# A diffusion layer on one Trainium2 core: the mixers' output product in seven products, and twelve first products ahead

## The chip, the cores and the metric

The kernel runs on one core of a Trainium2 chip. Its engines work from queues of their own: TensorE (PE) multiplies matrices, VectorE (DVE) and ScalarE (ACT) work on tiles element by element, GpSimd (POOL) adds some tiles and issues some transfers, SyncE (SP) issues most transfers. Engines wait for each other on semaphores. The metric is the device time of one execution in microseconds. Before the change it is 2686.76 us, the median of three runs (2683.47 to 2690.48).

## The reference, cut to what matters

One layer over 1024 latent tokens and 256 context tokens, all of width 1024: a half-step SwiGLU feed-forward (FFN), two token mixers side by side (short convolution and attention), merged by gates and multiplied by an output matrix, and a second FFN.

```python
x = x + 0.5 * ml[2] * swiglu(modulate(rms_norm(x, norm1_g), ml[0], ml[1]), ffn1_w_in, ffn1_w_out)
...
hx = modulate(rms_norm(x, norm2_g), ml[3], ml[4])
bg_l, cg_l, vc_l, q_l, k_l, v_l, gt_l = jnp.split(hx @ w_in, SPLITS, axis=-1)
...
x = x + ml[5] * ((g_conv * (y_conv @ w_bc) + g_attn * (o_attn @ w_ba)) @ w_out)
x = x + 0.5 * ml[8] * swiglu(modulate(rms_norm(x, norm3_g), ml[6], ml[7]), ffn2_w_in, ffn2_w_out)
return rms_norm(x, final_g)
```

`ml[0]` to `ml[8]` are nine vectors of modulation, `silu(c) @ w_mod + b_mod`, cut in nine. The context tokens go through the first FFN and the mixers' keys and values with the same weights.

## The kernel before, in words

**Layout and precision.** Activations lie transposed, 128 channels on the partitions and tokens along the row, in halves of 512 tokens: C0 and C1. Every factor of a matmul is split in a high and a low part, and three matmuls (high by high, high by low, low by high) make up one product of 128 x 128 by 128 x 512. ScalarE's cast makes the high part, DVE's subtraction the low one (`split`), so every operand costs one operation of each.

**Seven products for eight.** The large products with 1024 input channels (`Winograd`, L466) take a pair of column blocks of the weights, two halves of the inputs and two halves of the tokens, and form the four results from seven products of sums, in the order 1, 2, 6, 7, 4, 5, 3. `product(i)` takes one left part (the sums of weights, made by POOL; tiles s1 to s3 and raw, split into wl) and four right parts r(i) (the sums of normed inputs, made by DVE): 4 x 3 = 12 matmuls into one bank ps. `norm0` (L503) makes r1 and r2 from C0; `norm1` (L530) makes r6 and r5 from C1, then, in its last three steps, the right parts of products 7, 4 and 3 ("late" operands: each a `keep` of four tiles). `keep` is a cast on ScalarE and a subtraction on DVE.

**Starting ahead.** Products 1 and 2 need only C0. So `start` (L661) computes the first sums u and c of the first 9 pairs (AH2 for the mixers, AH3 for the second FFN; 12 for the first, through `start_together`), one pair after another, while the norm of C1 is made. Two pairs stay in the chip, the others are written to memory (`put_aside`, tiles uc and ucd, which have four buffers in the pool of weights, tag wh) and loaded again by `fetch` (L727) one pair ahead, into tiles u and c of the pool of small tiles (`ttile`, 11 buffers for everything temporary of 128x512). With one step of `norm1` for each pair (two for the first), all nine, the late ones too, are run within `start`. `second` (L743) adds products 6, 7 and 4, with calls for steps that are left (`run(self.late, 4)`); `third` (L755) adds 5 and 3.

**Row products.** The FFNs' second matrices go through `row_products` (L795): again seven products, each over all 11 pairs of hidden rows (tiles hid, rh, rl), into four banks at a time. When a product ends, `add` adds its four banks to x on DVE, at once.

**Modulation beside it.** `later_mod` (L262) multiplies the vectors that are needed later on DVE, from tiles rawm; its steps are run between pairs (`STEPS`, `late_steps`). After the last load it lets four (WAIT) and six steps pass idle before and after the accumulator is split (tiles macc, acch, accl).

**The mixers' end.** `merge(j, ch)` (L1640) multiplies the attention's output (`o_parts`, split in whole rows of 1024 by `split_output`, L1544: tiles oh and ol) by column block j of `w_ba` and gates it. It splits the merged rows into mh and ml. Then a loop over both halves and eight column blocks of `w_out` (L1714 to L1739) multiplies plainly: 8 x 3 = 24 matmuls for each block and half, into one bank, added to x by one operation on DVE. Each block is loaded and split once for each half of the tokens. Behind it `fast`, the second FFN's `Winograd`, starts (`norm0` within the loop's last blocks, `start` at L1841).

**What sets the order.** A scheduler that simulates the engines' timelines orders each engine's queue. Instructions issued while `strict[0]` is true, and matmuls marked `pinned`, keep their program order. Each queue is then worked in order, so that what is late at the head of DVE's or ScalarE's queue holds up everything behind it.

Of the kernel before, what the change touches and what calls it, by code (L numbers as in the profile page):

```python
# [49 lines left out]
def tile_dit_layer(  # L50
# [211 lines left out]
    def later_mod(m, halves=(0, 1), streams=None):  # L262
# [3 lines left out]
        for half in halves:  # L266
# [32 lines left out]
            yield  # L299
# [166 lines left out]
    class Winograd:  # L466
# [26 lines left out]
        def modulated(self, out, k, ch, pr):  # L493
            dve.tensor_mul(out=out, in0=self.xs(k, ch), in1=pr)
            self.shifted(out, k)

# [6 lines left out]
        def norm0(self, in_place=False):  # L503
# [8 lines left out]
            for i in range(2):  # L512
                for k in range(4):
                    h = self.h0[k][:, i]
                    self.modulated(h, k + 4 * i, C0, pr)
                    self.keep(1 + i, k, h)
                yield

# [51 lines left out]

        def lefts(self, pairs, side_from):

            def cols(src):
                t = wpool.tile([P, SLOT], F32, tag="raw", name=uniq("raw"), bufs=3)
                load(t[:].rearrange("p (k n) -> p k n", n=P), src.rearrange("(k p) n -> p k n", p=P))
                return t[:, :512], t[:, 512:]
# [9 lines left out]
            def parts(src):  # L586
                tag = "wh" if self.side_from and self.n_left in WH else "wl"
                self.n_left += 1
                t = wpool.tile([P, 2, 512], F32R, tag=tag, name=uniq(tag), bufs=W_BUFS)
                split(src, t[:, 0], t[:, 1], self.lo_eng)  # L590
                return t
# [11 lines left out]
            else:  # L603
                for a, _ in pairs[:n]:
                    yield from map(parts, cols(a))
# [689 lines left out]
    def after1(i, k):  # L1295
# [23 lines left out]
        if i == 3 and k in (0, 4):  # L1319
            run(norms2, 1)  # L1320
# [605 lines left out]
```

## Time and profile before

| | us |
|---|---|
| median of three runs | 2686.76 |
| the profiled execution | 2688.7 |
| its span, from first to last instruction | 2686.9 |
| PE busy | 2643.4 |
| weight loads of PE (PEld) busy | 2236.0 |
| DVE busy | 2007.1 |
| ScalarE busy | 1166.1 |
| POOL busy | 521.3 |

The program's stages lie in the profile so: first FFN's first product from about 30 us, its second product from 680, the mixers' products from 895, attention to 1850, the merges and the output product to 2054, then the second FFN. A page gives the busy time and its share of the span for each engine. A row of a timeline has the start, the length, the engine, the line, the operation, the tile written and the tiles read, how many alike follow each other, and in brackets the idle time before and what ended it. A row of waits names who waited, then after the arrow the tile that it waited for, and the sum, the count and the longest. All instructions have the line of one helper, so tiles and operations tell them apart. Matmuls overlap: one of 512 columns shows a duration near 390 ns, while the next starts much sooner.

### The profile page before, as it was taken

What the parts mean: (1) busy time and instruction counts of PE and PEld (TensorE: products, weight loads), DVE (VectorE), ACT (ScalarE), POOL (GpSimd) and SP (SyncE); (2) the same over time, 40 slices, a digit from 0 to 9 for tenths busy, and PEclk for the clock granted to TensorE, in tenths of its full rate; (3) what the DMA queues carried; (4) which work ended last, traced back from release to release, by engine and by line L of the source; (5) the groups of instructions that cost most, each with busy time, mean ns of one, the idle gap of its engine ahead of it and who ended that gap; (6) DMA issues with size and microseconds to landing.
All of it is one profiled execution on the core that took longest, in us unless ns stands there. A gap on an engine that the chain in (4) does not pass through costs nothing.

```text
span 2686.9 us, 37399 instructions
## 1 busy us (share of the span) xinstructions
PE 2643.4 (98%) x13593; PEld 2236.0 (83%) x13593; DVE 2007.1 (75%) x3356; ACT 1166.1 (43%) x2317; POOL 521.3 (19%) x409
## 2 busy tenths in 40 slices
PE   8999999999999999999999999999999999999998
PEld 5788898888788877888999888877888888888888
DVE  5888888786887889877488666775458875667875
ACT  6633543333454632333244666674236333334543
POOL 1244012121110044232033111000001533230200
PEclk9999999999999999999999999999999999999998
DMA  7655653346973445433213211002524543228731
GB/s 267 236 180 166 223 184 124 109 130 240 293 169 102 149 137 165 134 114 116 97 48 103 95 62 49 24 25 78 167 85 146 184 145 99 83 90 305 165 83 63
DMA packets 369920, 364.84 MB, mean 136 GB/s; under 512 B 27830, under 2 KB 261448, under 8 KB 369736
## 3 DMA queue, kind: packets, MB, share of 16 engines
q1 hardware_dynamic: 360712, 345.17, 39.0%
q0 software_dynamic: 9024, 17.30, 4.0%
q8 instruction: 106, 1.74, 0.3%
q14 instruction: 78, 0.64, 0.1%
HBM read 296.30 MB, written 66.06 MB: 135 GB/s over the span
## 4 chain that ended last, share of the span: by engine, by line
PE 88%; DVE 6%; DMA 2%; ACT 2%; issue 1%; SPq 1%; POOL 0%; DVEq 0%; ACTq 0%; POOLq 0%
PE ps L88 73%; PE po L88 7%; PE pt L88 7%; DMA rawm<-in_w_mod_dram 1%; DVE macc L88 1%; DVE wl L88 1%; SPq L88 1%; DVE xb L88 0%; DVE r L88 0%; ACT r L88 0%; DMA raw<-in_ffn_w_in_dram 0%; DMA xtok<-in_ctx_dram 0%; DVE ol L88 0%; DVE x L88 0%; DVE pts L88 0%
## 5 line engine op out<-in xcount | busy, mean ns | idle before, releaser
L88 PE MATMUL ps<-r,wl 128*128 128x512 f32 x5232 | 1213.4, 392 | 11.6 <-ACT wl L88 6.8
L88 PEld LDWEIGHTS ps<-r,wl 128*128 128x128 f32 x5232 | 983.9, 189 | 220.0 <-ACT wl L88 9.0
L88 ACT CAST wl<-s 128x512 fp32r<-128x512 f32 x256 | 158.0, 620 | 338.3 <-PE ps L88 266.6
L88 POOL TENSOR_TENSOR s<-raw 128x512 f32<-128x512 f32 x64 | 92.4, 1444 | 993.8 <-PE ps L88 346.6
L88 ACT CAST wl<-raw 128x512 fp32r<-128x512 f32 x286 | 176.4, 619 | 250.0 <-PE ps L88 160.6
L88 DVE TENSOR_TENSOR wl<-raw,wl 128x512 fp32r<-128x512 f32 x284 | 202.6, 717 | 68.3 <-ACT wl L88 64.7
L88 DVE TENSOR_TENSOR wl<-s,wl 128x512 fp32r<-128x512 f32 x256 | 231.8, 906 | 12.3 <-ACT wl L88 10.7
L88 POOL TENSOR_TENSOR s<-raw,s 128x512 f32<-128x512 f32 x64 | 99.8, 1560 | 363.9 <-DVE wl L88 354.4
L88 DVE SCALAR_TENSOR_TENSOR macc<-rawm,silu_c,macc 128x512 f32<-128x512 f32 x168 | 137.9, 837 | 9.5 <-DMA rawm<-in_w_mod_dram 9.1
L88 PE MATMUL ps<-wh,r 128*128 128x256 f32 x768 | 141.6, 285 | 0.0
L88 DVE TENSOR_TENSOR pts<-pt,pts 128x512 fp32r<-128x512 f32 x160 | 108.8, 687 | 39.4 <-ACT pts L88 38.4
L88 DVE TENSOR_TENSOR u<-u,ps 128x512 f32<-128x512 f32 x168 | 114.2, 680 | 28.5 <-PE ps L88 28.4
L88 DVE TENSOR_REDUCE m<-ps 128x1 f32<-128x512 f32 (+1 forms) x192 | 110.9, 596 | 31.0 <-PE ps L88 30.3
L88 ACT CAST pts<-pt 128x512 fp32r<-128x512 f32 x160 | 93.2, 593 | 88.7 <-PE pt L88 86.8
L88 ACT CAST rh<-hid 128x512 fp32r<-128x512 f32 x132 | 81.6, 621 | 112.2 <-PE ps L88 96.2
L88 PE MATMUL ps<-rh,wl 128*128 128x512 f32 x360 | 122.0, 389 | 0.0
L88 PEld LDWEIGHTS ps<-wh,r 128*128 128x128 f32 x768 | 120.6, 192 | 0.0
L88 ACT CAST wh<-raw 128x512 fp32r<-128x512 f32 (+1 forms) x88 | 69.3, 795 | 103.0 <-PE ps L88 79.5
L88 PE MATMUL po<-pts,vh 128*128 128x512 f32 x256 | 110.5, 437 | 1.5 <-ACT pts L88 1.5
L88 DVE TENSOR_TENSOR rl<-hid,rh 128x512 fp32r<-128x512 f32 x132 | 90.1, 686 | 26.5 <-ACT rh L88 13.5
L88 PE MATMUL ps<-wl,r 128*128 128x256 f32 x384 | 108.8, 283 | 0.0
L88 PE MATMUL ps<-kl,qs 128*128 128x512 f32 x384 | 105.3, 397 | 0.0
(298 smaller groups left out, 5068.1 us busy)
## 6 DMA issues: line engine op xcount, KB each, us to landing
raw<-in_ffn_w_in_dram SPq DMA_DIRECT2D x125, 512.0 KB
raw<-in_ffn_w_out_dram SPq DMA_DIRECT2D x72, 512.0 KB
rawm<-in_w_mod_dram SPq DMA_DIRECT2D x128, 256.0 KB
raw<-in_w_in_dram SPq DMA_DIRECT2D x61, 512.0 KB
hid<-hd SPq DMA_DIRECT2D x40, 512.0 KB
ws<-in_ffn_w_out_dram POOLq DMA_DIRECT2D x30, 512.0 KB, 6.6
ucd<-uc SPq DMA_DIRECT2D x22, 512.0 KB
hd<-c SPq DMA_DIRECT2D x38, 256.0 KB
```

What stands on the lines that cost most here:

```text
L88: inst = getattr(self.engine, name)(*args, **kw)
```

## The change

1. **The output product** becomes a `Winograd` of its own, `OutColumns`: four pairs of column blocks, seven products each, over merged rows instead of normed inputs. Its right parts are made as the merges end (`place`, `given`); products 1 and 2 of all four pairs are run first (`firsts`), then 6, 7 and 4 of all (`seconds`), then 5 and 3 (`fifth`, `last`). Each block of `w_out` is loaded once. The merges now run all of C0, then all of C1 in the order 0, 4, 1, 5, 2, 6, 3, 7, and load the columns of `w_ba` for each half. The squares of C0 are summed as they come.
2. **The start ahead**: AH3 goes from 9 to 12; `start` runs pairs in twos (product 1 of both, then product 2 of both), and the left parts are fetched in that order.
3. **Late operands**: of the last three steps of `norm1`, the first (product 7) still runs in `start`, the second (product 4) now stands behind product 6 and the third (product 3) behind product 4, both in program order (`late_operands`). The first FFN's `start` runs fewer of the steps of its norm ahead as well.
4. **Fetched first products** lie in the four wh buffers, in one transfer, and no longer in two small tiles.
5. **Row products**: the four banks of a product are added behind the first group's sums of the next product, in program order.
6. **Modulation**: no idle steps; a split stands behind the last load of its vector; `STEPS` is smaller, and the steps are run in thirds between the products of a pair.
7. **Attention's output** is split in halves of 512.

The core of the diff:

```diff
-STEPS = (0, 4, 4, 4, 5, 5, 5, 5, 5, 5, 5, 2, 12)
-WAIT = 4
+STEPS = (0, 3, 3, 3, 3, 3, 3, 4, 4, 4, 4, 1, 8)
 AH1, HALVES, WH = 12, 8, (4, 5, 6, 7, 12, 13, 14, 15, 20, 21, 22, 23)
-RESIDENT, AH2, AH3 = 2, 9, 9
+RESIDENT, AH2, AH3 = 2, 9, 12
...
-            for _ in range(WAIT):
-                yield
-            parts = []
-            for acc in accs:
+            for acc, v in zip(accs, streams):
                 ah, al = ttile("acch", dt=F32R), ttile("accl", dt=F32R)
                 split(acc, ah, al)
-                parts.append((ah, al))
-            for _ in range(6):
                 yield
-            for (ah, al), v in zip(parts, streams):
...
-            for i in range(self.n_ahead):
-                t = wpool.tile([P, 2, 512], F32, tag="wh", name=uniq("uc"), bufs=W_BUFS)
-                u, c = t[:, 0], t[:, 1]
-                act.copy(out=u, in_=self.product(1))
-                run(norm, 2 if i == 0 else 1)
-                dve.tensor_add(out=c, in0=u, in1=self.product(2))
-                if i < RESIDENT:
-                    self.started.append((u, c))
-                else:
-                    self.put_aside(t)
-            run(norm, 9 - self.n_ahead)
+            n, ts = self.n_ahead, []
+            for j in range(0, n, 2):
+                for i in range(j, min(j + 2, n)):
+                    t = wpool.tile([P, 2, 512], F32, tag="wh", name=uniq("uc"), bufs=W_BUFS)
+                    act.copy(out=t[:, 0], in_=self.product(1))
+                    ts.append(t)
+                for i in range(j, min(j + 2, n)):
+                    run(norm, 2 if i == 0 else 1 if i < 5 or i == self.n_ahead - 2 else 0)
+                    t = ts[i]
+                    dve.tensor_add(out=t[:, 1], in0=t[:, 0], in1=self.product(2))
+                    if i < RESIDENT:
+                        self.started.append((t[:, 0], t[:, 1]))
+                    else:
+                        self.put_aside(t)
...
-                u, c = ttile("u"), ttile("c")
-                for i, t in enumerate((u, c)):
-                    load(t, self.started[0][:, i])
-                self.started[0] = u, c
+                t = wpool.tile([P, 2, 512], F32, tag="wh", name=uniq("uc"), bufs=W_BUFS)
+                load(t[:], self.started[0][:])
+                self.started[0] = t[:, 0], t[:, 1]
...
-            run(self.late, 4)
+            self.late_operands(1)
             dve.tensor_add(out=v, in0=u, in1=self.product(7))
             if self.side:
                 self.side(0, self.left())
             dve.tensor_sub(out=b, in0=v, in1=self.product(4))
-            run(self.late)
+            self.late_operands()
             return v, b
+
+        def late_operands(self, n=None):
+            strict[0] = True
+            run(self.late, n)
+            strict[0] = False
...
+    class OutColumns(Winograd):
+
+        def __init__(self, pairs):
+            super().__init__(None, None, None, 0, pairs)
+            self.h0, self.h1 = [None] * 4, [None] * 4
+
+        def lefts(self, pairs, side_from):
...
+            for j in range(len(pairs)):
+                if j == 1:
+                    b.append(self.cols(pairs[3][1]))
+                (a0, a1), (b0, b1) = a[j], b[j]
+                s1, s2, s3 = ttile("s1"), ttile("s2"), ttile("s3")
+                pool.tensor_add(out=s1, in0=b0, in1=b1)
+                pool.tensor_sub(out=s2, in0=s1, in1=a0)
+                pool.tensor_sub(out=s3, in0=a0, in1=b0)
...
+        def firsts(self):
+
+            self.uc = []
+            for _ in range(4):
+                t = atile("uc", (P, 2, 512))
+                act.copy(out=t[:, 0], in_=self.product(1))
+                dve.tensor_add(out=t[:, 1], in0=t[:, 0], in1=self.product(2))
+                self.uc.append((t[:, 0], t[:, 1]))
+                yield
+
+        def seconds(self, j):
+
+            u, v = self.uc[j]
+            b = ttile("b")
+            dve.tensor_add(out=u, in0=u, in1=self.product(6))
+            dve.tensor_add(out=v, in0=u, in1=self.product(7))
+            dve.tensor_sub(out=b, in0=v, in1=self.product(4))
+            return b
+
+        def fifth(self, j):
+
+            u, v = self.uc[j]
+            p5 = self.product(5)
+            dve.tensor_add(out=v, in0=v, in1=p5)
+            dve.tensor_add(out=u, in0=u, in1=p5)
+
+        def last(self, j):
+
+            u, _ = self.uc[j]
+            dve.tensor_add(out=u, in0=u, in1=self.product(3))
...
+        chain, results = None, []
+
+        def add_results():
+            while results:
+                i, ps = results.pop()
+                for o, ch in to[i]:
+                    for d in range(4):
+                        add(o + d, ch, ps[d])
+                after(i, rows.n)
...
+                add_results()
...
+            results.append((i, ps))
...
+            t = o_parts[hd, ch] = atile("o", (P, 2, 512), F32R)
+            split(q_f[hd][:, ch[1] : ch[1] + 512], t[:, 0], t[:, 1])
...
-        dve.tensor_add(out=ga, in0=ga, in1=z)
-        split(ga, m_hi[j][:, o : o + 512], m_lo[j][:, o : o + 512])
+        dve.tensor_add(out=merged.place(j % 4, j // 4, ch), in0=ga, in1=z)
+        merged.given(j % 4, j // 4, ch)
...
+    for j in range(2, KD):
+        run(merge(j, C0))
+    for j in (0, 4, 1, 5, 2, 6, 3):
+        run(merge(j, C1))
+    merged.prefetch(2)
+    run(merge(7, C1))
...
+    firsts = merged.firsts()
+    run(firsts, 1)
+    residuals(C0, (0, 1, 4, 5))
+    run(firsts)
+    residuals(C0, (2, 3, 6, 7))
+    for j in range(4):
+        add2(2 * j, C0, merged.uc[j][1])
+        add2(2 * j + 1, C0, merged.seconds(j))
+        if j == 1:
+            residuals(C1, range(KD))
+    merged.prefetch(8)
+    strict[0] = True
+    merged.fifth(0)
+    merged.last(0)
+    run(first, 1)
...
```

Three places of DVE's queue show how the order moves.

**The mixers' start.** Here the last of the pairs started ahead ends (its sum is `uc_8955` before, `uc_8915` after), and the first weights of the next products follow (wl). `r` from `t` and `r` from `h` are the low halves of late operands. Before:

```order
L88 TENSOR_TENSOR r_1526_8821<-t_1511_8756,r_1526_8821 128x512
L88 TENSOR_TENSOR r_1534_8863<-t_1473_8587,r_1534_8863 128x512
L88 TENSOR_TENSOR r_1535_8866<-t_1485_8642,r_1535_8866 128x512
L88 TENSOR_TENSOR r_1536_8869<-t_1498_8699,r_1536_8869 128x512
L88 TENSOR_TENSOR uc_8955<-uc_8955,ps_8976 128x512
L88 TENSOR_TENSOR r_1537_8872<-t_1511_8756,r_1537_8872 128x512
L88 TENSOR_TENSOR r_1545_8914<-h_1472_8586,r_1545_8914 128x512
L88 TENSOR_TENSOR r_1546_8917<-h_1484_8641,r_1546_8917 128x512
L88 TENSOR_TENSOR r_1547_8920<-h_1497_8698,r_1547_8920 128x512
L88 TENSOR_TENSOR r_1548_8923<-h_1510_8755,r_1548_8923 128x512
L88 TENSOR_TENSOR wl_8936<-s_1552_8931,wl_8936 128x512
L88 TENSOR_TENSOR wl_8956<-s_1553_8932,wl_8956 128x512
```

After:

```order
L87 TENSOR_TENSOR r_1529_8874<-t_1466_8573,r_1529_8874 128x512
L87 TENSOR_TENSOR r_1530_8877<-t_1482_8648,r_1530_8877 128x512
L87 TENSOR_TENSOR r_1531_8880<-t_1491_8685,r_1531_8880 128x512
L87 TENSOR_TENSOR r_1532_8883<-t_1508_8762,r_1532_8883 128x512
L87 TENSOR_TENSOR uc_8915<-uc_8915,ps_8936 128x512
L87 TENSOR_TENSOR wl_8896<-s_1536_8891,wl_8896 128x512
L87 TENSOR_TENSOR wl_8916<-s_1537_8892,wl_8916 128x512
L87 TENSOR_TENSOR wl_8933<-raw_8888,wl_8933 128x512
L87 TENSOR_TENSOR wl_8952<-s_1535_8890,wl_8952 128x512
L87 TENSOR_TENSOR uc_8490<-uc_8490,ps_8966 128x512
L87 TENSOR_TENSOR r_1558_8980<-t_1466_8573,r_1558_8980 128x512
L87 TENSOR_TENSOR r_1559_8983<-t_1482_8648,r_1559_8983 128x512
```

Before, eight low halves made from t and four made from h stand ahead of the first wl. After, four stand there; the next four follow behind the sum with product 6 (`uc_8490`), and those from h behind product 4.

What PE does at this place after the change (`ps_8936` is the last first product, `ps_8966` product 6, `ps_8996` product 7, `ps_9023` product 4, `ps_9052` product 5; x3 are the three matmuls of one right part):

```order
L87 MATMUL ps_8936<-r_1434_8398,wl_8855 128x512 x3
L87 MATMUL ps_8966<-r_1469_8583,wl_8896 128x512 x2
L87 MATMUL ps_8996<-r_1529_8874,wl_8916 128x512 x2
L87 MATMUL ps_8966<-r_1469_8583,wl_8896 128x512
L87 MATMUL ps_8966<-r_1485_8658,wl_8896 128x512 x3
L87 MATMUL ps_8966<-r_1494_8695,wl_8896 128x512 x3
L87 MATMUL ps_8966<-r_1511_8772,wl_8896 128x512 x3
L87 MATMUL ps_8996<-r_1529_8874,wl_8916 128x512
L87 MATMUL ps_8996<-r_1530_8877,wl_8916 128x512 x3
L87 MATMUL ps_8996<-r_1531_8880,wl_8916 128x512 x3
L87 MATMUL ps_8996<-r_1532_8883,wl_8916 128x512 x3
L87 MATMUL ps_9023<-r_1558_8980,wl_8933 128x512
```

Four matmuls, on the high halves of two weights, stand between the end of the first products and the first use of a weight's low half.

**The second FFN's start, at the end of its first products.** `uc_19809` before and `uc_20004` after are the last pair's sum; wl are the weights of the products that follow. Before:

```order
L88 TENSOR_TENSOR r_3532_19675<-t_3517_19610,r_3532_19675 128x512
L88 TENSOR_TENSOR r_3540_19717<-t_3479_19441,r_3540_19717 128x512
L88 TENSOR_TENSOR wl_19790<-s_3558_19785,wl_19790 128x512
L88 TENSOR_TENSOR r_3541_19720<-t_3491_19496,r_3541_19720 128x512
L88 TENSOR_TENSOR wl_19810<-s_3559_19786,wl_19810 128x512
L88 TENSOR_TENSOR uc_19809<-uc_19809,ps_19830 128x512
L88 TENSOR_TENSOR wl_19827<-raw_19782,wl_19827 128x512
L88 TENSOR_TENSOR r_3542_19723<-t_3504_19553,r_3542_19723 128x512
L88 TENSOR_TENSOR wl_19846<-s_3557_19784,wl_19846 128x512
L88 TENSOR_TENSOR r_3543_19726<-t_3517_19610,r_3543_19726 128x512
```

After:

```order
L87 TENSOR_TENSOR r_3586_19785<-nt_19781,r_3586_19785 128x512
L87 TENSOR_TENSOR r_3587_19789<-nt_19780,r_3587_19789 128x512
L87 TENSOR_TENSOR uc_20004<-uc_20004,ps_20066 128x512
L87 TENSOR_TENSOR r_3633_20032<-t_3541_19586,r_3633_20032 128x512
L87 TENSOR_TENSOR r_3634_20035<-t_3557_19661,r_3634_20035 128x512
L87 TENSOR_TENSOR r_3635_20038<-t_3566_19698,r_3635_20038 128x512
L87 TENSOR_TENSOR r_3636_20041<-t_3583_19775,r_3636_20041 128x512
L87 TENSOR_TENSOR wl_20015<-s_3629_20010,wl_20015 128x512
L87 TENSOR_TENSOR wl_20044<-s_3630_20011,wl_20044 128x512
L87 TENSOR_TENSOR wl_20063<-raw_20007,wl_20063 128x512
L87 TENSOR_TENSOR wl_20082<-s_3628_20009,wl_20082 128x512
L87 TENSOR_TENSOR uc_19503<-uc_19503,ps_20087 128x512
```

Before, the keeps of two late operands and the weights alternate on both sides of the last sum. After, the sum, four keeps and then the weights follow each other.

**The first FFN's second matrix, where a product ends.** `x_... <- ps_...,gate_l` are the four additions of a result, wl and wh the next weights, rl and hid right parts and sums of hidden rows. Before:

```order
L88 TENSOR_TENSOR hid_6558<-hid_6559,hid_6558 128x1024
L88 SCALAR_TENSOR_TENSOR x_1159_6794<-ps_6582,gate_l,x_1159_6794 128x512
L88 SCALAR_TENSOR_TENSOR x_1160_6796<-ps_6583,gate_l,x_1160_6796 128x512
L88 SCALAR_TENSOR_TENSOR x_1161_6798<-ps_6584,gate_l,x_1161_6798 128x512
L88 SCALAR_TENSOR_TENSOR x_1162_6800<-ps_6585,gate_l,x_1162_6800 128x512
L88 TENSOR_TENSOR hid_6560<-hid_6560,hid_6558 128x1024
L88 TENSOR_TENSOR rl_7015<-hid_6566,rh_7014 128x512
L88 TENSOR_TENSOR wl_6920<-raw_6918,wl_6920 128x512
L88 TENSOR_TENSOR wh_6941<-raw_6918,wh_6941 128x512
```

After:

```order
L87 TENSOR_TENSOR rl_6999<-hid_6550,rh_6998 128x512
L87 SCALAR_TENSOR_TENSOR x_1151_6778<-ps_6566,gate_l,x_1151_6778 128x512
L87 SCALAR_TENSOR_TENSOR x_1152_6780<-ps_6567,gate_l,x_1152_6780 128x512
L87 TENSOR_TENSOR wl_6900<-raw_6898,wl_6900 128x512
L87 SCALAR_TENSOR_TENSOR x_1153_6782<-ps_6568,gate_l,x_1153_6782 128x512
L87 SCALAR_TENSOR_TENSOR x_1154_6784<-ps_6569,gate_l,x_1154_6784 128x512
L87 TENSOR_TENSOR wh_6921<-raw_6898,wh_6921 128x512
L87 TENSOR_TENSOR hid_6544<-hid_6544,hid_6542 128x1024
```

Before, four additions, a sum over 1024 columns and a right part stand ahead of the weight `wl_6920`. After, two of the additions do (the weight is `wl_6900`), and the other two and the sum stand behind it.

More of the change, by code (lines that the diff above doesn't have):

```diff
@@ L603, in lefts @@
             else:
-                for a, _ in pairs[:n]:
-                    yield from map(parts, cols(a))
+                for j in range(0, n, 2):
+                    two = [cols(a) for a, _ in pairs[j : min(j + 2, n)]]
+                    for half in range(2):
+                        for a in two:
+                            yield parts(a[half])
             for j, (wa, wb) in enumerate(pairs):
@@ L920, in row_products @@
                 sums(i, g)
+                add_results()
                 strict[0] = False
                 after(i, k)
-            for o, ch in to[i]:
-                for d in range(4):
-                    add(o + d, ch, ps[d])
-            after(i, rows.n)
+            results.append((i, ps))
+        if not halves:
+            add_results()
         if halves:
@@ L1245, in tile_dit_layer @@
                     do(step, half1.left())
-                run(steps, 3)
+                run(steps, 2)
                 if i % 2 == 0:
@@ L1651, in merge @@
         terms = [
[L1652 removed]
+            (w[0][:, k], w[1][:, k], o_parts[k, ch][:, 0], o_parts[k, ch][:, 1]) for k in range(KD)
         ]
@@ new lines, in tile_dit_layer @@
+    merged.prefetch(8)
[3 more added lines that the diff above has]
+    run(first, 1)
+    merged.fifth(1)
+    run(first, 2)
+    merged.last(1)
+    run(first, 1)
+    merged.fifth(2)
+    run(first, 1)
+    merged.last(2)
+    run(first, 1)
+    fast.prefetch(2)
+    merged.fifth(3)
+    run(first, 2)
+    merged.last(3)
+    run(first)
+    fast.prefetch(4)
+    for j in range(4):
+        for i in range(2):
+            add2(2 * j + i, C1, merged.uc[j][i])
+    strict[0] = False
```

147 lines of the change are left out of this document (86 added, 61 removed).

## The prediction

> **What bounds the kernel now.** Read first is the page: busy shares, chain, clock.
>
> ```profile
> PE 2643.4 (98%) x13593; PEld 2236.0 (83%) x13593; DVE 2007.1 (75%) x3356; ACT 1166.1 (43%) x2317; POOL 521.3 (19%) x409
> ...
> PE 88%; DVE 6%; DMA 2%; ACT 2%; issue 1%; SPq 1%; POOL 0%; DVEq 0%; ACTq 0%; POOLq 0%
> ```
>
> TensorE (PE) is busy nearly throughout and holds 88% of the chain that ended last. But a matmul's shown duration overlaps the next one's, so what one fewer is worth must come from an unbroken stretch. The chain has one just ahead of the second FFN's product:
>
> ```profile
> 1861.04 135.32 PE ps L88 x597
> 1996.36 0.79 PE pt L88 x8
> 1997.14 7.19 PE ps L88 x31
> 2004.34 0.44 PE pt L88 x4
> ```
>
> 597 matmuls of 512 columns in 135.32 us are **0.2267 us each**, with no wait among them. The output product, which the change rewrites, lies in this stretch and the next, so a matmul removed here takes its pitch off the end, as long as the next stage's operands keep up. A half product (one left part, 12 matmuls) is 2.72 us.
>
> The second view is the waits of PE, by stretch. They add up to little outside the start-up, but they come in knots, and one view shows the largest:
>
> ```profile
> PE ps L88 <- ACT wl L88: 6.6, 2, 5.1
> PE ps L88 <- DVE wl L88: 1.1, 1, 1.1
> ```
>
> This is 900 to 1100 us, total, times and longest. The third view, PE's timeline, shows where, and that a wait costs more than its length:
>
> ```profile
> 943.57 11.68 PE L88 MATMUL ps<-r,wl 128*128 128x512 f32 x38 [5.05 <-ACT wl L88]
> ...
> 1057.68 0.73 PE L88 MATMUL ps<-r,wl 128*128 128x512 f32 x2 [1.51 <-ACT wl L88]
> 1059.48 10.86 PE L88 MATMUL ps<-r,wl 128*128 128x512 f32 x34 [1.07 <-DVE wl L88]
> ```
>
> The 38 matmuls behind the first wait should take 38 x 0.2267 = 8.6 us and took 11.68: 3.1 more. The 34 behind the third should take 7.7 and took 10.86: 3.2 more. The granted clock is down in just these stretches (the third number from the end of each row of the table by stretches):
>
> ```profile
> 900.00:1000.00 100.00, 94.95 (x414) 78.13 (x414) 87.95 (x153) 45.01 (x81) 33.02 (x19) 0.97 0.47 150
> 1000.00:1100.00 100.00, 97.43 (x416) 79.47 (x415) 90.94 (x132) 31.40 (x56) 36.40 (x25) 0.97 0.53 169
> ```
>
> So knot one, at the mixers' start, costs 5.05 + 3.1 = **8.1 us**, and knot two 1.51 + 1.07 + 3.2 = **5.8 us**.
>
> **The sum, part by part.**
>
> *Output product.* Before:
>
> ```profile
> L88 PE MATMUL ps<-mh,wl 128*128 128x512 f32 x128 | 49.9, 390 | 0.0
> L88 PE MATMUL ps<-mh,wh 128*128 128x512 f32 x128 | 49.9, 390 | 0.0
> L88 PE MATMUL ps<-ml,wh 128*128 128x512 f32 x128 | 49.8, 389 | 0.0
> ```
>
> 3 x 128 = 384. After: 4 pairs of column blocks x 7 products x 12 = 336. 48 x 0.2267 = **-10.9 us**. The squares of C0 now have sums of their own over ones, eight short matmuls as in the row 1996.36: **+0.8**. What rides along is hidden. The stretch's row in the same table, and the costliest kind of POOL's sums:
>
> ```profile
> 1850.00:2100.00 250.00, 249.86 (x1119) 206.61 (x1118) 158.09 (x236) 96.15 (x146) 19.38 (x12) 1.00 0.44 141
> ```
> ```profile
> L88 POOL TENSOR_TENSOR s<-raw,s 128x512 f32<-128x512 f32 x64 | 99.8, 1560 | 363.9 <-DVE wl L88 354.4
> ```
>
> VectorE (DVE) was busy 158 of 250 us and gets some 60 operations of about 0.6 us (36 us) here; GpSimd (POOL), busy 19, gets 16 sums of 1.56 us (25 us); ScalarE, busy 96, gets casts for fewer than 60. The last merges are DVE's tightest place: I count about 10.2 us of work per 10.9 us of four products there. But what is late behind them (nine operations, 5.4 us) is read first by the first product 6, eight products (21.8 us) later. Without that cover it would cost those 5.4 us.
>
> [...]
>
> *Mixers' start.* DVE's timeline around the 5.05 us wait:
>
> ```profile
> 937.93 4.29 DVE L88 TENSOR_TENSOR r<-t,r 128x512 fp32r<-128x512 f32 x7
> 942.14 0.67 DVE L88 TENSOR_TENSOR uc<-uc,ps 128x512 f32<-128x512 f32 x1
> 942.74 0.68 DVE L88 TENSOR_TENSOR r<-t,r 128x512 fp32r<-128x512 f32 x1
> 943.34 2.48 DVE L88 TENSOR_TENSOR r<-h,r 128x512 fp32r<-128x512 f32 x4
> 945.75 1.28 DVE L88 TENSOR_TENSOR wl<-s,wl 128x512 fp32r<-128x512 f32 x2
> ```
>
> Twelve low halves of late operands stand ahead of the first weight of the new stage, and their twelve casts stand ahead of its cast on ScalarE. After, the first four (for product 7) stand there alone; the other eight come behind product 6's and product 4's sums. Then the queue is: the last first product's sum (0.6), the weight's low half (0.6), ready some 1.3 to 1.4 us after that product ends. PE has four matmuls without it (0.9 us): a wait of about 0.5 in place of 8.1, too short for the clock. **-7.6**, from -8.1 to -4 (if four keeps are still in the way: 2.5 us of DVE, and the clock follows). What is late next are the moved operands. Those of product 4 are ready 6.6 us into the stage, by a count of DVE's queue, and are reached at 8.9; those of product 3 at 14.5 and 15.2. They fit, with 0.7 us to spare.
>
> *FFN1's second product, where one result is added and the next weights are split.* PE's wait there, and DVE's queue:
>
> ```profile
> PE pt L88 <- DVE wl L88: 1.7, 1, 1.7
> ```
> ```profile
> 701.81 2.72 DVE L88 SCALAR_TENSOR_TENSOR x<-ps,gate_l,x 128x512 f32<-128x512 f32 x4
> 704.45 1.21 DVE L88 TENSOR_TENSOR hid<-hid,hid 128x1024 f32<-128x1024 f32 x1
> 705.58 0.68 DVE L88 TENSOR_TENSOR rl<-hid,rh 128x512 fp32r<-128x512 f32 x1
> 706.18 0.68 DVE L88 TENSOR_TENSOR wl<-raw,wl 128x512 fp32r<-128x512 f32 x1
> ```
>
> After, two of the four adds (2 x 0.68) and the 1.21 us sum stand behind that weight, 2.6 us against a wait of 1.7: **-1.7**.
>
> *Knot two.* What POOL, whose sums ScalarE then casts to weights, waited for there:
>
> ```profile
> POOL s L88 <- DVE accl L88: 10.4, 1, 10.4
> ```
>
> POOL waited 10.4 us for a split of a modulation accumulator, which holds one of the small buffers that POOL's sums also rotate through. After, the split follows the last load at once (ten idle steps are gone) and the fetched first products live elsewhere, so the buffers come free sooner. The trace can't show the new rotation. Bounds: nothing, if another buffer holds it, and all 5.8; I take **-4**, nearer to all, since both causes of holding go.
>
> *Attention's output split* goes from 128x1024 to 128x512 operations:
>
> ```profile
> L88 DVE TENSOR_TENSOR ol<-q,oh 128x1024 fp32r<-128x1024 f32 x5 | 6.1, 1222 | 1.8 <-ACT oh L88 1.8
> ```
>
> A half instead of the whole stands ahead of PE's short waits, though the halves are often adjacent: -0.5, from -2 to 0.
>
> *The second FFN's start.* Its norm's reciprocal roots come after the sums 1996.36; before, 31 matmuls (7.19 us) cover them till the transposes at 2004.34; after, one product of 12 (2.72 us) does. The last operation of the roots on DVE:
>
> ```profile
> 1999.16 0.17 DVE L88 SCALAR_TENSOR_TENSOR rs_y<-rs_t,rs_y 128x4 f32<-128x4 f32 x1
> ```
>
> The sums end at 1997.15 and the roots 2.2 us later, so 0.5 us is left of the 2.72, and the norm's low halves, which follow on DVE, are late for the first product 2: **+1**, from 0 to 2.5. At the end of its twelve first products DVE must do the last sum and four low halves of product 7's operands, then the weight. By
>
> ```profile
> 2070.65 3.09 DVE L88 TENSOR_TENSOR r<-t,r 128x512 fp32r<-128x512 f32 x5
> ```
>
> (0.62 each) that is 6 x 0.62 = 3.7 us, while PE has seven matmuls (1.6 us) to go on with: **+2**, from 0 to 6 (if the clock follows as in knot two).
>
> *FFN1's first start* (pairs in twos, three fewer idle steps, four product-7 keeps ahead of four weights): nearly the same work in another order beside 48 matmuls of cover: +1; no row shows this order, so I take half of knot one for bounds, -4 to +4.
>
> Sum: -10.9 + 0.8 - 7.6 - 1.7 - 4 - 0.5 + 1 + 2 + 1 = -19.9.
>
> ```profile
> span 2686.9 us, 37399 instructions
> ```
>
> The profiled execution took 2688.7 us for this span, and the median of the runs is 2686.76, 1.9 below that execution; so 2686.8 - 19.9 = **2667 us**.
>
> **The rivals.**
>
> *The stalls move* (2675 to 2680). The matmuls go, but knot two stays (+4) and the new wait of about 2 us before the second FFN's product 6 brings the clock down (+3 to +4), or the mixers' start keeps half its wait (+4): 2667 + 8 = 2675, with all three 2679. For it: knot two shows a lower clock behind two gaps of 1.51 and 1.07 us, so 2 us can be enough. Against it: there it took two gaps, and here I count one. The Trainium skill (TensorE: Matmul & The Clock Gate, Part 1) says that the clock halves after an idle window of about 3.4 us. The gap of 5.05 agrees; the pair of 1.51 and 1.07, 1.8 us apart, doesn't, and the measurement decides. By the rule the new 2 us wait would cost no clock and the forecast stands.
>
> *Slower: first products set aside come back too late* (2695). First products now run in twos, and two of the four buffers that hold their pairs stay resident, so a buffer is written to memory and used again in the time from one pair's second product to the first product two pairs on: 5.44 us, less the 0.7 of the sum, against 8.16 before. If the write lands later, each use of a buffer is late by the difference, and ScalarE, in order, holds up the weight casts behind the copy. Ten pairs in the second FFN and seven in the mixers use a buffer five and three times again. For a landing L the loss is 8 x (L - 4.7), less twice the 5.4 us that weights cast ahead cover in each stage (four, of which I count half as still to be used). At L = 6.6 this is 4 us, at 9.5 it is 28 and the kernel is slower: 2667 + 28 = 2695; even is reached near 8.5, where the loss is the 20 us gained. For a price, the nearest row is a load of the same size; and ScalarE's waits ahead of the copies:
>
> ```profile
> ws<-in_ffn_w_out_dram POOLq DMA_DIRECT2D x30, 512.0 KB, 6.6
> ```
> ```profile
> ACT uc L88 <- PE ps L88: 17.1, 13, 3.9
> ```
>
> The copies waited for PE, and no row of ScalarE's waits has them wait for a transfer, so before they landed within 10.9 - 0.7 - 2.7 = 7.5 us. That speaks against 8.5.
>
> *It brings nothing* (2685 to 2688): only if the seven products don't lie on the path, that is, if the next stage's operands set the end of this one, as they do in no row from 1861 to 2054.
>
> **How the numbers follow.** Forecast case 0.68, its own range 2655 to 2676. The stalls move 0.23. Slower 0.06, nothing 0.03. The low end takes every term at its best: -10.9 + 0.8 - 8.1 - 1.7 - 5.8 - 2 + 0 + 0 - 4 = -31.7, 2655. The high end reaches past the moving stalls, with -4 at the mixers, 0 at knot two, +6, +2.5 and +4: -10.9 + 0.8 - 4 - 1.7 + 12.5 = -3.3, 2684. A measurement of this kernel tells about 0.3% (8 us) from no change: faster means below 2678.7. The forecast case and three fifths of the second give 0.82, the rest of the second and nothing 0.12, slower 0.06.
>
> **What would show it.** Right: PE's matmuls fall by 48 with the pitch unchanged in the output product; no wait above 1 us at the mixers' start and clock 1.00 in 900 to 1000; no wait at the product change near 707; a wait of 1.5 to 2.5 us ahead of the second FFN's first product 6. Wrong: rows of ScalarE's copies waiting for a transfer of first products; a low clock near the second FFN's start; POOL's wait for the accumulator still near 1050; DVE, not PE, in the chain within the last merges.

## The result and the profile after

The changed kernel takes 2714.69 us (median of five runs, 2709.24 to 2717.89) against 2686.76 for the kernel before: a ratio of **1.0103**, 95% interval 1.0086 to 1.0119. It is slower by 28 us where 2667 was forecast. Its profiled execution took 2711.1 us for a span of 2709.3. The page:

```profile
span 2709.3 us, 37431 instructions
...
PE 2645.2 (98%) x13553; PEld 2224.9 (82%) x13553; DVE 2087.6 (77%) x3438; ACT 1180.6 (44%) x2360; POOL 559.2 (21%) x425
...
PE 75%; DVE 11%; DMA 3%; issue 2%; ACT 1%; SPq 0%; ACTq 0%; DVEq 0%
```

PE is as busy as before, but holds 75% of the chain in place of 88%. The waits of PE, first over the whole span, then from 2100 to 2240 us:

```profile
PE ps L87 <- ACT wl L87: 19.1, 12, 4.4
PE ps L87 <- DVE wl L87: 12.0, 14, 2.1
```
```profile
PE ps L87 <- ACT wl L87: 7.2, 5, 2.0
PE ps L87 <- DVE r L87: 0.8, 2, 0.6
```

Before, the same two kinds were 8.0 and 3.0 us, and there was none in the second stretch. To place them all, I add up by stretch how much later than its pitch (0.2267 us for 512 columns, 0.120, 0.109 and 0.112 for the smaller forms) each matmul's successor starts. This counts the lower clock too.

| stretch (us) | before | after | change | forecast |
|---|---|---|---|---|
| first FFN, 100 to 400 | 6.9 | 20.3 | +13.4 | +1 |
| its second product, 670 to 800 | 4.4 | 3.2 | -1.2 | -1.7 |
| mixers' products, 900 to 1100 | 14.4 | 9.8 | -4.6 | -11.6 |
| attention, 1500 to 1855 | 16.5 | 15.0 | -1.5 | -0.5 |
| output product, second FFN's first products, 1930 to 2060 | 0.1 | 3.7 | +3.6 | +1 |
| end of those, 2060 to 2110 | 0.7 | 8.9 | +8.2 | +2 |
| pairs set aside, 2110 to 2260 | 0.0 | 14.4 | +14.4 | 0 |
| all else | 28.7 | 28.7 | 0 | 0 |

The stalls grow by 32.3, the matmuls' own time falls by 10.0 (the forecast's -10.9 and +0.8): +22.3, and the spans differ by 22.4. So the saving is there, and two stretches in which the prediction saw little, where pairs that were set aside come back, take it and more. The stretches are the same microseconds in both kernels, and after the change the later stages begin some 10 us later: a wait near an edge can fall into the next stretch.

The chain within the last such stretch shows how (start, length, what):

```profile
2179.28 1.71 DVE uc L87
2181.00 1.99 DMA hd<-uc
2183.00 4.77 DMA uc<-ucd
2188.50 0.58 ACT wl L87
2189.10 0.69 DVE wl L87
```

A pair's result is stored (hd<-uc), only then is another pair fetched (uc<-ucd), and then come a weight's high and low half. PE's weights have nothing to do with the fetched pair, which comes three pairs further on (four buffers, and the one that is freed takes the fourth pair after). What joins the two is ScalarE's queue, in its timeline and in its waits from 2080 to 2245:

```profile
2187.93 0.63 ACT L87 ACTIVATE uc<-uc 128x512 f32<-128x512 f32 x1 [8.98 <-DMA uc<-ucd]
2188.47 0.60 ACT L87 CAST wl<-s 128x512 fp32r<-128x512 f32 x1
```
```profile
ACT uc L87 <- DMA uc<-ucd: 49.4, 8, 9.0
```

The order of that queue after the change, around the activation of such a fetched pair (`uc_20657`; the pair at work is `uc_20318`), is

```
L87 CAST wl_20456<-s_3697_20365 128x512
L87 ACTIVATE uc_20657<-uc_20657 128x512
L87 CAST wl_20483<-s_3717_20478 128x512
L87 CAST wl_20506<-s_3718_20479 128x512
L87 CAST wl_20524<-raw_20475 128x512
L87 CAST wl_20551<-s_3716_20477 128x512
L87 ACTIVATE uc_20318<-uc_20318 128x512
```

The activation (silu of the pair's first result) depends on nothing but the fetch, and the scheduler puts it ahead of the next weights' casts and of the second activation of the pair at work. On the chip the fetch waits for a buffer, ScalarE waits 9 us for the fetch, and PE for the casts:

```profile
2181.85 5.63 PE L87 MATMUL ps<-r,wl 128*128 128x512 f32 x24
2189.12 3.22 PE L87 MATMUL ps<-r,wl 128*128 128x512 f32 x7 [1.64 <-ACT wl L87]
```

The seven matmuls behind the wait take 3.22 us instead of 1.6: the granted clock is down, as the row of these 6 us in the table by stretches shows (0.74, third from the end).

```profile
2187.00:2193.00 6.00, 4.36 (x13) 2.83 (x12) 3.90 (x5) 3.17 (x6) 1.66 (x1) 0.74 0.16 49
```

The other waits that the account below needs, in PE's timeline:

```profile
954.82 31.27 PE L87 MATMUL ps<-r,wl 128*128 128x512 f32 x133 [2.47 <-ACT wl L87]
...
1955.27 42.95 PE L87 MATMUL ps<-r,wl 128*128 128x512 f32 x188 [2.10 <-DVE wl L87]
...
2095.40 12.94 PE L87 MATMUL ps<-r,wl 128*128 128x512 f32 x43 [4.36 <-ACT wl L87]
```

They stand at the mixers' start (before, the row of 5.05 us at 943.57), at the output product's first products and at the end of the second FFN's first products. The chain into the last of them (start, length, what) begins with the store of a pair that is set aside:

```profile
2082.18 5.91 DMA ucd<-uc
2088.18 0.58 ACT uc L87
2088.77 0.73 ACT h L87
...
2092.13 2.69 ACT r L87 x5
2094.83 0.53 ACT wl L87
2095.40 2.07 PE ps L87 x4
```

ScalarE's copy of a first product (uc) waits 2.65 us for that store. Behind it in the queue come a step of the norm (h), the casts of its last results (r), and only then the weights.

### The profile page after: what moved, and what is told of

The parts are those of the page before. It is cut to its first block, busy times and chain, and to the rows that moved or that the text cites. A ratio compares the mean times of both kernels' runs of the same rounds, so it can differ in the third digit from the quotient of the medians.

```text
span 2709.3 us, 37431 instructions
## 1 busy us (share of the span) xinstructions
PE 2645.2 (98%) x13553; PEld 2224.9 (82%) x13553; DVE 2087.6 (77%) x3438; ACT 1180.6 (44%) x2360; POOL 559.2 (21%) x425
## 4 chain that ended last, share of the span: by engine, by line
PE 75%; DVE 11%; DMA 3%; issue 2%; ACT 1%; SPq 0%; ACTq 0%; DVEq 0%
PE ps L87 61%; PE po L87 8%; PE pt L87 7%; DVE wl L87 2%; DVE uc L87 2%; DVE macc L87 1%; DMA uc<-ucd 1%; DMA hd<-uc 1%; DVE r L87 1%; DVE nt L87 1%; DVE v L87 1%; DMA rawm<-in_w_mod_dram 1%; DVE y L87 0%; ACT wl L87 0%; DVE b L87 0%
## 5 line engine op out<-in xcount | busy, mean ns | idle before, releaser
L87 PE MATMUL ps<-r,wl 128*128 128x512 f32 x5496 | 1287.1, 393 | 35.9 <-ACT wl L87 19.1
L87 PEld LDWEIGHTS ps<-r,wl 128*128 128x128 f32 x5496 | 1031.0, 189 | 270.6 <-ACT wl L87 27.1
L87 POOL TENSOR_TENSOR s<-raw 128x512 f32<-128x512 f32 x68 | 103.3, 1520 | 893.7 <-DMA raw<-in_ffn_w_in_dram 294.3
L87 ACT CAST wl<-raw 128x512 fp32r<-128x512 f32 x298 | 183.5, 619 | 218.1 <-PE ps L87 143.0
L87 DVE TENSOR_TENSOR wl<-raw,wl 128x512 fp32r<-128x512 f32 x296 | 210.0, 716 | 70.0 <-ACT wl L87 67.3
L87 POOL TENSOR_TENSOR s<-raw,s 128x512 f32<-128x512 f32 x68 | 106.0, 1559 | 450.9 <-DVE wl L87 445.5
L87 DVE SCALAR_TENSOR_TENSOR macc<-rawm,silu_c,macc 128x512 f32<-128x512 f32 x168 | 150.2, 912 | 12.7 <-DMA rawm<-in_w_mod_dram 12.4
L87 POOL TENSOR_TENSOR s<-raw,raw 128x512 f32<-128x512 f32 x68 | 111.4, 1638 | 5.2 <-DVE macc L87 3.0
L87 DVE TENSOR_TENSOR uc<-uc,ps 128x512 f32<-128x512 f32 x148 | 99.6, 677 | 12.7 <-PE ps L87 12.7
L87 POOL TENSOR_TENSOR s<-s,raw 128x512 f32<-128x512 f32 x68 | 105.2, 1547 | 10.6 <-DVE macc L87 3.6
```

The source lines that it names most:

```text
L87: inst = getattr(self.engine, name)(*args, **kw)
```

## The experiments

Theory F: the fetch in the wh buffers is what costs. Theory S: the modulation's steps between the products are. Each run is given with its ratio to runs of the kernel before on the same chip.

**1. The fetch into a large tile.**

```diff
-                t = wpool.tile([P, 2, 512], F32, tag="wh", name=uniq("uc"), bufs=W_BUFS)
+                t = atile("uc", (P, 2, 512))
```

> The changed kernel with one edit altered: a fetched pair of first products lies in a large tile of the general pool instead of one of the four wh buffers, still in one transfer. Theory F (the fetch waits for the store of the pair that had the buffer, and ScalarE, in order, waits for its landing ahead of weight casts): the waits of PE in 200 to 400 and 2100 to 2250 us go, some 25 of the 29 us by which PE's stalls there exceed those of before, so about 2690 us (2683 to 2697). Theory S (the modulation steps, which now run between products and without idle steps, delay DVE): nothing changes there, 2710 to 2718.

2704.2 us, 1.0067 (1.0051 to 1.0083). The stalls of 100 to 400 fall from 20.3 to 10.5, but those of 2110 to 2260 are 16.6. The chain there reads as before:

```profile
2168.61 1.98 DMA hd<-uc
2170.66 4.51 DMA uc<-ucd
2175.20 0.04 issue
2175.24 0.06 ACT uc L87
```

In the general pool, too, the fetch begins as a store ends. The time lies between the ranges of the two theories: the first FFN loses half of its stalls, the second none.

**2. The kernel before, with only the fetch in the wh buffers.**

> The kernel before with only the fetch of first products moved into the four wh buffers, in one transfer. Theory F: PE stalls in the first and the second FFN's consumption of set-aside pairs; with 9 pairs ahead in the second FFN and 12 in the first, +10 to +25 us on 2686.8. Theory S: within 4 us of before.

2693.2 us, 1.0025 (1.0014 to 1.0035): +6.7, less than the 10 to 25 expected. 8.0 us of stall in 2110 to 2260, none new in the first FFN. The mechanism works alone, but costs the changed kernel more.

**3. The kernel before, with only the output product changed** (`OutColumns`, the halved split, the norm's first half by chunks).

> The kernel before with only the output product in seven products (with the split of attention's output in halves and the norm's first half in steps of one chunk, on which it rests). The prediction's term: -10.9 for 48 matmuls, +0.8 for the sums over ones, up to +1 at the second FFN's start: about 2677 us. The rival seen in the changed kernel's trace: DVE operations beside POOL's sums take 1.7 instead of 0.6 us, and 2 to 4 us are lost again where the output product begins (2679 to 2681).

2696.4 us, 1.0042 (1.0027 to 1.0057): 19 us more than expected. PE's timeline:

```profile
2080.48 49.73 PE L88 MATMUL ps<-r,wl 128*128 128x512 f32 x212 [14.70 <-ACT wl L88]
```

The seven products finish the second half of the tokens only with their last ones, so its norm starts later than in the plain loop, and nine pairs' first products don't cover it.

**4. The kernel before, with only the late operands behind products 6 and 4.**

```diff
-                run(norm, 2 if i == 0 else 1)
+                run(norm, 2 if i == 0 else 1 if i < 5 or i == self.n_ahead - 2 else 0)
...
-            run(self.late, 4)
+            self.late_operands(1)
...
-            run(self.late)
+            self.late_operands()
```

> The kernel before with only the late operands moved behind products 6 and 4 (9 pairs ahead, one pair after another as before). The prediction's term: the knot at the mixers' start (8.1 us) falls to 0.5 us; the second FFN's start gets its four product-7 keeps ahead of the weight, +2: about 2681 us. A rival: the strict order of the late operands puts new waits in the first pairs of the three stages and takes the gain back, 2686 to 2690.

2682.1 us, 0.9987 (0.9977 to 0.9997), as expected. Stall of 900 to 950: 8.3 to 2.6; of 950 to 1040: 0.1 to 2.3. The second FFN's start shows no new wait.

**5. The changed kernel, with the activation in program order.**

```diff
+        strict[0] = ch == C0
         act.activation(out=a, in_=a, func=AF.Silu)
+        strict[0] = False
```

> The changed kernel with ScalarE's activation of a pair's first result (silu of c) kept in program order, so that it stands behind its own pair's product 4 and not, as the scheduler puts it, next to the fetch of that pair, two pairs ahead of its use. The four wh buffers stay. Theory F2 (what costs is that the activation waits for the fetched pair at the head of ScalarE's queue, ahead of weight casts): the stalls of the second FFN from 2110 to 2260 (14.4 us) and most of the first FFN's from 200 to 400 (17.6 against 5.3 before) go, 2687 to 2697. Theory F (the buffers themselves are short, so first products come late to PE): no change, 2710 to 2718.

(By the queue above it is three pairs ahead, not two.)

**2686.0 us, 0.9995 (0.9986 to 1.0004)**: 1.1% below the changed kernel by the ratios, with the same buffers and the same fetch. 2110 to 2260 falls from 14.4 to 3.4, 100 to 400 from 20.3 to 11.5. ScalarE no longer waits for a fetch in that stretch; the longest of its waits from 2100 to 2260 are

```profile
ACT wl L87 <- PE ps L87: 46.0, 26, 2.6
ACT uc L87 <- DVE uc L87: 32.2, 10, 8.2
```

So late buffers alone don't cost the time; the place of the activation in ScalarE's queue turns their lateness into waits of PE.

**6. The changed kernel, fetching into two small tiles as before.**

> The changed kernel with the fetch as before: two transfers into two of the small tiles. In the kernel before, ScalarE waited for these too, but no more than 6.5 us, and PE did not wait. Theory F2: the small tiles come free sooner than a pair's store, so the activation waits less and the stalls of 2110 to 2260 fall from 14.4 to 0 to 5; about 2697 to 2705. If the 11 small tiles are short for twelve pairs ahead, the stalls stay or move to POOL's sums: 2710 or more.

2689.6 us, 1.0010 (1.0000 to 1.0019), better than expected. 2110 to 2260: 0.1. The scheduler still places the activation, and it still waits for fetches, but less:

```profile
ACT c L87 <- DMA c<-ucd: 9.8, 7, 3.4
```

**7. As 3, with 12 pairs ahead.**

> As the kernel before with only the output product changed, but 12 pairs ahead in the second FFN (one pair after another, fetched as before). There, with 9 ahead, PE waited 14.7 us at 2080 for the norm of the second half of the tokens, which the seven products finish only at their end. Theory N: three pairs more give 16.3 us of cover, the wait goes nearly whole, 2696.4 - 14 = 2682 or less. Rival: the norm's work on DVE takes longer beside twelve pairs' weight splits, or POOL's sums slow DVE, and a wait of 4 us or more stays: 2685 to 2690.

2685.0 us, 0.9994 (0.9984 to 1.0004): the theory had 2682 or less, the rival 2685 to 2690. A wait of 3.77 us stays of 14.70 (5.7 us of stall): three pairs more are not quite enough. This is the changed kernel's knot at 2090 without its buffers and without its order of starts, and here no copy of ScalarE waits for a store.

**8. As 6, with the modulation's steps as before.**

> As the changed kernel with the fetch as before, and the modulation's steps also as before (between pairs, with the idle steps, the larger counts). Theory S: the stalls on low halves of weights on DVE in 240 to 290 (3.8 us in 6 waits) and 997 to 1075 (4.3 us in 5) go, some 8 us below the run that differs only in the steps. Otherwise the same within 3 us of that run.

2681.9 us, 0.9979 (0.9969 to 0.9988): 7.7 below run 6, as expected, but all of it in one of the two places named: 100 to 400 falls from 12.0 to 3.8, while 950 to 1100 stays (6.5 both). Theory S holds for the first FFN.

**9. As 5, with 11 pairs ahead in the mixers and 14 in the second FFN.**

> The changed kernel with the activation in program order (as in the run before that had 2686.0) and more pairs ahead: 11 in the mixers, 14 in the second FFN. Theory N (the norm of the second half of the tokens isn't done when the first products end, so PE waits at the end of each start): the 4.4 us wait at the second FFN's product 6 with its lower clock (9.0 us of stall in 2060 to 2110) and the 2.5 us at the mixers' start (3.4 in 900 to 950) go; -9 to -12, about 2675. Rival W (what ends those starts is the write of set-aside pairs and the weights' splits, which grow with the pairs ahead): the waits stay, 2683 or more.

2677.5 us, 0.9971 (0.9961 to 0.9982): by the ratios 6.4 below run 5, less than the 9 to 12 expected. 2060 to 2110: 9.0 to 1.0; 900 to 950: 3.4 to 0.1. But 1040 to 1100 rises from 2.6 to 6.9, so 900 to 1100 stays at 9.8: in the mixers the wait only moves. Compared by PE's timeline, run 5 and run 9 at the end of the second FFN's first products:

```profile
2081.74 13.05 PE L87 MATMUL ps<-r,wl 128*128 128x512 f32 x43 [4.36 <-ACT wl L87]
```
```profile
2059.64 42.09 PE L87 MATMUL ps<-r,wl 128*128 128x512 f32 x185
2101.92 0.96 PE L87 MATMUL ps<-r,wl 128*128 128x512 f32 x3 [0.18 <-DVE r L87]
```

So both starts wait for the norm, and more first products cover it. The stores of set-aside pairs are more than before, and ScalarE's copies still wait 2.1 us for them in 2030 to 2112, but PE no longer does. The run changes both numbers of pairs at once, so what each is worth alone stays open.

**10. As 8, with 5's order and 9's pairs ahead.**

> As the changed kernel, with the fetch and the modulation's steps as before, the activation in program order, and 11 and 14 pairs ahead. If the parts add up: 2681.9 (fetch and steps as before) less 6 to 8 for the second FFN's start and 3 to 4 for the mixers': 2670 to 2674, below both kernels. If the small tiles run short with more pairs aside: 2680 or more.

2680.2 us, 0.9978 (0.9969 to 0.9987): the parts don't add up. 1040 to 1100 has 15.5 us of stall, two waits on weights of 3.72 and 5.95 us. POOL, whose sums become those weights, waited 21.9 us in two waits there for fetched tiles (c<-ucd): the small tiles run short, as the rival said.

**11. The kernel before, with only 5's order.**

> The kernel before with only ScalarE's activation of a pair's first result kept in program order. Theory F2 says that the wait at the head of ScalarE's queue cost PE nothing there (ScalarE waited 40.4 us in 13 waits for fetched tiles, PE had no stall between 2110 and 2600): within 3 us of before. If it shortens the kernel by more, the wait cost something already.

2682.5 us, 0.9989 (0.9980 to 0.9998): 3.0 below before by the ratio. The stall of 200 to 300 goes from 5.2 to 0.7. The early activation cost a little there already.

**12. As 9, with the sums of the output product's first two pairs on DVE.**

```diff
+                adder = dve if j < 2 else pool
...
-                pool.tensor_add(out=s1, in0=b0, in1=b1)
+                adder.tensor_add(out=s1, in0=b0, in1=b1)
```

> As the run with the activation in program order and more pairs ahead (2677.5), but the weights' sums of the output product's first two pairs are made on DVE, not on POOL. Theory C (DVE's low halves take 1.1 us longer each while POOL adds, and that makes the 1.8 us wait of PE at the output product's first products): no DVE operation of 128x512 over 1 us in that stretch (1930 to 1956); the eight added sums cost DVE 4.8 us and the lengthened ones give back 4 to 5, so the wait stays at 1 to 2.5 us and the time within 3 us. Rival (the long operations come from something else, such as the transfers): they stay long, the wait grows to about 6 us, 2681 or more.

**2672.9 us, 0.9955 (0.9938 to 0.9972)**, the lowest of all and below both kernels; its interval overlaps run 9's. First run 9's DVE and POOL, then run 12's DVE, at the same place of the program:

```profile
1936.12 0.68 DVE L87 TENSOR_TENSOR r<-nt,r 128x512 fp32r<-128x512 f32 x1
1936.72 3.48 DVE L87 TENSOR_TENSOR r<-t,r 128x512 fp32r<-128x512 f32 x2
1940.13 1.78 DVE L87 TENSOR_TENSOR r<-nt,r 128x512 fp32r<-128x512 f32 x1
```
```profile
1936.62 1.33 POOL L87 TENSOR_TENSOR s<-raw 128x512 f32<-128x512 f32 x1 [6.50 <-DVE t L87]
1938.03 1.63 POOL L87 TENSOR_TENSOR s<-s,raw 128x512 f32<-128x512 f32 x1
1939.62 1.74 POOL L87 TENSOR_TENSOR s<-raw,raw 128x512 f32<-128x512 f32 x1
```
```profile
1934.94 0.68 DVE L87 TENSOR_TENSOR r<-nt,r 128x512 fp32r<-128x512 f32 x1
1935.55 1.29 DVE L87 TENSOR_TENSOR r<-t,r 128x512 fp32r<-128x512 f32 x2
1936.75 0.68 DVE L87 TENSOR_TENSOR r<-nt,r 128x512 fp32r<-128x512 f32 x1
```

The same three operations take 5.2 us with POOL adding and 1.9 without. PE's wait there, 1.84 us in run 9, is gone and not merely kept, so the expectation was too careful. The two runs differ in this edit alone.

## Why the prediction was wrong

**The step that failed** is the one on knot two and its companion, the fetch. The prediction moved the fetched first products "elsewhere" and counted only what that frees, the small tiles (-4). It didn't work out what the fetch waits for in its new place, nor what is queued behind its reader on ScalarE. The profile before had the row that warns, ScalarE's waits for a fetched tile, and the prediction doesn't speak of it:

```profile
ACT c L88 <- DMA c<-ucd: 40.4, 13, 6.5
```

With buffers that come free later the longest wait grows from 6.5 to 9 us, past the 5.4 us that the prediction itself gave to the weights cast ahead. The price is 29 us by the ratios of run 5 and the changed kernel, 24 of them stalls, about 20 of these in 100 to 400 and 2110 to 2260. It takes both, the late buffers and the early activation: run 6, with the old tiles, is rid of 25 us too.

**The rival on set-aside pairs** had the buffers, the in-order queue and the weight casts right, and "slower" was given 0.06. It put the wait on the write, in the starts. Its sign, ScalarE's copies waiting for a transfer of first products, did come: 3.7 us in two waits at the second FFN's start, the longer one in the chain above. But the large cost is not there: it lies at the reading back, and run 9, with more pairs written, has no wait of PE over 0.3 us left at the ends of the starts.

With the order mended (run 5) the kernel is only as fast as before. Its matmuls have the -10.0, but its stalls are 8.0 above those of before, where the forecast had them 9.8 below. What follows is the rest.

**The output product** gave its matmuls (-10.0 in the table). But the norm of the second half now starts at the very end (run 3: 14.70 us with nine pairs ahead). With twelve, my 2 us, reckoned from DVE's queue as if it had caught up, measured 8.2: the wait is 4.36 us, for weights cast behind the norm's last results, and the clock takes most of the rest. More cover removes it (run 9). The store of a set-aside pair delays the norm there by up to 2.65 us; without any such wait 3.77 us stay (run 7), which suggests that most of it is the norm's own, but no run divides the 4.36.

**POOL's sums** were called hidden because POOL was idle. They were, but not what they do to DVE: 1.1 us longer for each low half beside them. That makes the wait at the output product's start (2.10 us; 1.84 in run 9, gone in run 12), a term I had at 0.

**The mixers' start** was to give 7.6 us, with a wait of 0.5 us left of 5.05. The wait is 2.47 us (the row at 954.82; the stage begins 11 us later than before). From 900 to 1040 the stalls fall by 1.3 alone, from 8.4 to 7.1, since new waits on low halves of weights follow, the longest 1.72 us near 999. Moving the operands helps (run 4: 8.3 to 2.6, with 2.3 behind it). What was left out is the norm itself: its last low halves and casts stand ahead of the first weights, and with 11 pairs ahead the wait is gone (run 9), though 1040 to 1100 then takes as much. DVE's norm ran beside POOL's sums there too; what that costs at this place was not tried.

**Knot two** (1040 to 1100) fell from 6.0 to 2.7, against -4 forecast. POOL's long wait for the accumulator, which the prediction blamed, is gone with the fetch's buffers alone (3.0, run 2) and with the new steps alone (4.0, run 6). But the knot varies with neither changed, from 3.7 (run 11) to 6.4 (run 3), where that wait stays at about 10 us, and it is 6.9 in run 9 without that wait. So the size came out near, and the cause is not shown.

**The product change** (-1.2 against -1.7) and **attention's split** (-1.5 against -0.5) held. **The first FFN's start** was bounded at +4, and its stretch cost 13.4, where the set-aside pairs come back: keeping the activation in order takes 8 to 9 away (run 5), the old steps 8 in a kernel with the old fetch (run 8); the two overlap.

On the clock: behind the 4.36 us wait 43 matmuls took 12.94 us, 3.2 more than their pitch gives. The rival of moving stalls had asked whether a wait of 2 us is enough for that. It can be: the wait of 1.64 us, 16 us behind one of 1.95, was followed by a lower clock, though for less, 1.6 us in seven matmuls. But the 2.47 us at the mixers' start was not: the granted clock of 950 to 986 is 1.00. So the length of a wait alone doesn't tell. The Trainium skill (TensorE: Matmul & The Clock Gate, Part 1) names an idle window of about 3.4 us, by which the wait of 1.64 us would have cost its length only; the measurement differs.

## What to carry to other kernels

Ask of every tile that gets another buffer what its next writer waits for, and of every reader what stands behind it on its engine: a scheduler may put the reader early, right behind its transfer, and an in-order queue then makes others wait for data that they don't need. Keep such a reader in the place of its use. When a product is rearranged so that its results come all at the end, give the next stage more work that doesn't need them, and price the operations of DVE as they run beside POOL's, not alone. And when a wait is gone from a fixed stretch, look whether it has only moved into the next.

## What was not expected of the hardware

DVE's subtractions of two tiles in SBUF took 1.7 to 1.8 us beside POOL's additions and 0.6 to 0.7 without, run for run (3.48 against 1.29 for two). A sum of a tile with a matmul's bank stayed at 0.68 us in the middle of such an addition, here at the mixers' start of the changed kernel (DVE's and POOL's timelines):

```profile
946.94 0.68 DVE L87 TENSOR_TENSOR uc<-uc,ps 128x512 f32<-128x512 f32 x1
```
```profile
946.43 1.74 POOL L87 TENSOR_TENSOR s<-raw,raw 128x512 f32<-128x512 f32 x1
```

The Trainium skill (SBUF — State Buffer, Who interferes with whom) says that a DVE instruction with two inputs in SBUF contends with a GpSimd instruction that reads SBUF, and calls the lock on the ports that they share exclusive. Run 9's rows agree: the two later subtractions end at 1940.20 and 1941.91 us, each 0.5 to 0.6 us behind the end of an addition of POOL (1939.66 and 1941.36).
